# A streaming encoder layer on one core: the norm row stays in PSUM, the first tile's products are reordered, and output weights and gates are staged in other buffers

## The chip, the core and the metric

The kernel runs on 1 NeuronCore of one Trainium2 chip. The engines are TensorE (PE, with its weight loads as PEld), VectorE (DVE), ScalarE (ACT), GpSimd (POOL) and SyncE (SP, which issues all DMAs here). The metric is the device time of one execution in microseconds, as the median of several runs; lower is better.

## The reference

One layer of a hybrid encoder, for 2048 new frames and 64 frames of a running stream with a past of 4096. After a root-mean-square norm one combined projection gives ten column blocks; two branches (differential attention and retention) follow, each gated, projected, weighted by a sigmoid gate and summed; an output projection and the residual close the layer.

```python
h = rmsnorm(x, norm_g) @ w_in                      # 1024 -> 6144 columns
qa, ka, va, za, qb, kb, vb, zb, ga, gb = split(h)  # 512 each, ga and gb 1024
qa, ka = rmsnorm(qa, qn_g), rmsnorm(ka, kn_g)      # per head half of 64
ga, gb = sigmoid(ga + b_gate[0]), sigmoid(gb + b_gate[1])
oa = diff_attention(qa, ka, va)                    # 4 heads, chunk-causal, ALiBi
ob = retention(qb, kb, vb)                         # 4 heads, decay per head
oa = rmsnorm(oa, subln_g) * (1 - lam_init) * silu(za)
ob = rmsnorm(ob) * silu(zb)
m = ga * (oa @ w_o_diff) + gb * (ob @ w_o_ret)
y = x + m @ w_out
```

All inputs and outputs are 32-bit floats. The keys, the values and the retention state are outputs as well.

## The kernel before

**Products in three passes.** Each operand of a large product is split into a high part (fp32r) and the remainder: h is a cast on ScalarE, l = x - h a subtraction on VectorE or GpSimd. A product is then three passes on TensorE: high x high, high x low, low x high. So every weight piece is loaded by SP into a staging buffer, cast on ScalarE, subtracted on VectorE or GpSimd, and its staging buffer is free after that.

**Order of work.** The program is written as generators that a loop in Python runs by priority against estimated engine times (P, A, V, G, ld, and take and give for buffers); this fixes the order of TensorE, ScalarE and VectorE. The order on GpSimd and on SP comes from the framework's scheduler. Each engine then runs its list in order, and a DMA waits on SP for its buffer and also for the DMA eight places earlier.

**Start.** x_prep and x_norm load a tile of x (128 frames x 1024), take the sum of squares on ScalarE (L288), then the inverse root (Ln L291, Exp L292, and small VectorE steps L295 to L300 on one column), and scale x by it and by the norm row gn (L305). gn is norm_g spread over 128 partitions by a product with a matrix of ones (L271) and copied from PSUM into a row buffer (L273). x_tile transposes on TensorE (L319), and casts and subtracts into xh and xl (L326, L327). w_load loads w_in in pieces of 256 KB, w_split casts (L391) and subtracts them (on GpSimd L398, or VectorE L395); natural and mm_group multiply (L427). The first eight pieces have eight staging places (STAGE), of which the first and the last share a pool of three. Twelve small products of ones (L1607) run before x is there.

**Middle.** Projections, attention (z_stream) and retention are interleaved on TensorE until the projections of the second half end with the gate columns gb, which are stored from ev to gbT (L615). z_stream ends some 60 us before the projections; then load_wo loads both 512 x 1024 weights w_o in 32 pieces of 128 x 256 through the nine buffers of oz, and out_prep loads z and o of each branch in groups of 264 frames and forms o * silu(z), split into ogh and ogl (og_fin, L1330 to L1347).

**Output projection.** It starts when the last projection is done, since its buffers (pool p3b: w_out, the gates gt, m, xt, yt) lie where the projection's were. out_stream runs eight groups of 256 prompt frames and 8 sample frames. m_tile makes one of eight blocks of 128 columns for both branches in PSUM (tags mm and s, two buffers each; L1385 to L1387). m_fin multiplies both by their gates on VectorE (L1405), which frees the PSUM, adds them on GpSimd (L1409) and splits the sum (mh L1415, ml L1423). gate_prep loads a pair of gate tiles (ga and gb, 132 KB each) and applies the sigmoid (L1366). load_wout loads w_out in 32 pieces of 128 x 256; these and the gate pairs share the six buffers of gt. y_tile multiplies m by w_out (L1450 to L1452; 8 blocks of m x 2 halves of the columns x 3 passes), and y_fin adds x (L1464) and stores. A last y_tile serves the 64 sample frames.

Of the kernel before, what the change touches and what calls it, by code (L numbers as in the profile page):

```python
# [12 lines left out]
ALU = mybir.AluOpType  # L13
# [22 lines left out]
        "oz": 9, "og": 17, "gt": 6, "m": 18, "xt": 2, "yt": 2}  # L36
# [5 lines left out]
XFLY = 5  # L42
STAGE = ["ws", "ws", "ws", "ath", "ath", "atl", "atl", "ws"]
# [12 lines left out]
class Hybrid:  # L56
# [192 lines left out]
    def x_prep(self, half):  # L249
# [4 lines left out]
        gn = self.row("gn")  # L254
        jk = self.row("xjk")
        tiles = self.xtiles(half)
        left = [len(tiles)]
        for j, (src, r, seg, col) in enumerate(tiles):
            yield lambda: self.xfly < XFLY and (half > 0 or self.wloads >= min(4 * j, 8))
# [5 lines left out]
            if j == 0 and half == 0:  # L265
                tg = self.ld(self.gz[0:1, :], self.i["norm_g"][0:1, :], 4096)
                self.ld(self.ident, self.i["c_ident"], 1 << 16)
                for k in range(2):
                    sl = slice(512 * k, 512 * k + 512)
                    ps = self.psum("s")  # L270
                    nc.tensor.matmul(ps, self.ones, self.gz[:, sl], start=True, stop=True)  # L271
                    t = self.P(2048)
                    nc.vector.tensor_scalar_mul(gn[:, sl], ps, 128.0)  # L273
                    tg = self.V(512, t)
                self.give("row", tg)
# [5 lines left out]
        self.give("row", self.dve + LAT, 2)  # L281

    def x_norm(self, j, xt, jk, gn, t, tg, r, seg, col, left):
# [11 lines left out]
        nc.vector.tensor_scalar(ms, ss, 1.0 / D, EPS, op0=ALU.mult, op1=ALU.add)  # L295
        self.V(1, t)
        yield t2
        nc.vector.scalar_tensor_tensor(out=ms, in0=y, scalar=y, in1=ms, op0=ALU.mult, op1=ALU.mult)
        nc.vector.tensor_scalar(ms, ms, -0.5, 1.5, op0=ALU.mult, op1=ALU.add)
        nc.vector.tensor_mul(y, y, ms)  # L300
# [4 lines left out]
        nc.vector.scalar_tensor_tensor(out=xt, in0=xt, scalar=y, in1=gn[:r], op0=ALU.mult, op1=ALU.mult)  # L305
# [37 lines left out]
    def w_load(self):  # L343
        for half in range(2):
            for c0, wide in self.order[half]:
                for q in range(8 if wide else 4):
                    tag = STAGE[q] if self.wloads < 8 else "ws"
                    yield from self.take(tag)
                    pool = self.wp if tag == "ws" else self.ap
# [31 lines left out]
    def w_split(self):  # L381
        nc = self.nc
        nw = n = 0
        for c0, wide in self.order[0] + self.order[1]:
            for q in range(8 if wide else 4):
# [6 lines left out]
                t = self.A(512, self.pe)  # L392
                if wide and q % 2:
# [7 lines left out]
                if wide:  # L401
                    self.wq.append((h, l, t, tags))
                else:
                    self.wq.append((h[:, 0], l[:, 0], t, ()))
                    self.wq.append((h[:, 1], l[:, 1], t, tags))
# [12 lines left out]
    def mm_group(self, ps, n, us, wsl, x, wfirst, last):  # L418
        nc = self.nc
        seg, xsl = x  # L420
        for c in range(KC):
# [10 lines left out]
            if c % 2 and c < KC - 1:  # L432
                yield self.pe
# [1247 lines left out]
```

## Time and profile before

| what | value |
| --- | --- |
| runs | 2028.14, 2029.12, 2029.59 us; median 2029.12 |
| the profiled execution | 2029.37 us, of which 2027.6 us span |
| TensorE busy | 1991.4 us (98% of the span), 12406 passes |
| VectorE, ScalarE, GpSimd busy | 1003.2, 956.3, 410.5 us |
| DMA | 280.97 MB, mean 139 GB/s |
| mean granted TensorE clock | 0.995 |
| TensorE busy from 0 to 50 us, from 50 to 100 us | 41.81 us (clock 0.90), 48.86 us |
| TensorE busy from 100 to 1600 us | 1493.5 of 1500 us |
| TensorE busy from 1600 to 1650 us, from 1650 to 1700 us | 42.83 us (clock 0.97), 41.77 us (clock 0.93) |
| TensorE busy from 1700 to 2000 us | 49.90 us of each 50 |

How to read it: a line of the timeline gives start and duration in us, the engine, the line of the kernel, the operation, what it writes and from what, and, in brackets, how long the engine had been idle and what ended that. SPq is SP's queue of DMA issues. The span runs from the first to the last instruction; the profiled execution's own time has 1.8 us more.

### The profile page before, as it was taken

How to read it: one execution, taken by the hardware profiler on the slowest of the kernel's cores; microseconds unless marked ns; L12 is line 12 of the kernel's file. 1: busy time of each engine (PE TensorE's matmuls, PEld its weight loads, DVE VectorE, ACT ScalarE, POOL GpSimd, SP SyncE). 2: the span in 40 equal slices, each digit the busy share in tenths (PEclk: the TensorE clock that was granted, in tenths of full speed). 3: DMA queues.
4: the chain of work that ended last, by engine and by line, in shares of the span. 5: the costliest groups of instructions: out<-in, count | busy, mean ns of one | idle time of the engine just before them, and what ended most of it. 6: DMA issues, size and time to landing. Idle time of an engine off the chain costs nothing. (4 is left out here: it accounts for less than half of the span.)

```text
span 2027.6 us, 34426 instructions
## 1 busy us (share of the span) xinstructions
PE 1991.4 (98%) x12406; PEld 1787.8 (88%) x12406; DVE 1003.2 (49%) x2671; ACT 956.3 (47%) x2112; POOL 410.5 (20%) x385
## 2 busy tenths in 40 slices
PE   8999999999999999999999999999999979999999
PEld 6778999989998999999999888888888868888997
DVE  7453566543331421546856555645653455444442
ACT  6332676644332433535666655645653553333321
POOL 2110121121112222221211211122112443222210
PEclk8999999999999999999999999999999989999999
DMA  6646554344565463663352352553234664454531
GB/s 223 200 140 167 149 158 132 106 137 139 152 176 130 135 189 92 180 194 115 115 159 79 96 146 71 148 156 94 68 92 145 187 185 151 142 157 130 149 100 58
DMA packets 332573, 280.97 MB, mean 139 GB/s; under 512 B 64945, under 2 KB 300465, under 8 KB 332402
## 3 DMA queue, kind: packets, MB, share of 16 engines
q1 hardware_dynamic: 332402, 278.77, 46.9%
q8 instruction: 98, 1.61, 0.3%
q14 instruction: 73, 0.60, 0.1%
HBM read 187.19 MB, written 91.49 MB: 137 GB/s over the span
## 5 line engine op out<-in xcount | busy, mean ns | idle before, releaser
L427 PE MATMUL mm<-xh,wh 128*128 128x512 f32 (+2 forms) x1280 | 461.2, 360 | 0.0
L427 PE MATMUL mm<-xh,wl 128*128 128x512 f32 (+2 forms) x1280 | 451.6, 353 | 0.0
L427 PE MATMUL mm<-xl,wh 128*128 128x512 f32 (+2 forms) x1280 | 450.9, 352 | 0.0
L398 POOL TENSOR_TENSOR wl<-ws,wh 128x512 fp32r<-128x512 f32 x180 | 239.3, 1339 | 926.8 <-ACT wh L391 602.5
L427 PE MATMUL mm<-wh,xh 128*128 128x256 f32 (+3 forms) x872 | 276.6, 317 | 0.3 <-DVE tlo L558 0.3
L427 PE MATMUL mm<-wh,xl 128*128 128x256 f32 (+3 forms) x872 | 271.0, 311 | 0.0
L427 PE MATMUL mm<-wl,xh 128*128 128x256 f32 (+3 forms) x872 | 270.8, 311 | 0.0
L427 PEld LDWEIGHTS mm<-xh,wl 128*128 128x128 f32 x1280 | 241.0, 188 | 31.9
L427 PEld LDWEIGHTS mm<-xh,wh 128*128 128x128 f32 x1280 | 241.2, 188 | 29.7 <-issue 0.2
L427 PEld LDWEIGHTS mm<-xl,wh 128*128 128x128 f32 x1280 | 241.5, 189 | 29.0
L615 ACT COPY ev<-mm 128x512 f32<-128x512 f32 x140 | 71.6, 511 | 250.3 <-PE mm L427 232.1
L427 PEld LDWEIGHTS mm<-wh,xh 128*128 128x128 f32 (+1 forms) x872 | 164.6, 189 | 11.7 <-PE s L790 0.4
L427 PEld LDWEIGHTS mm<-wl,xh 128*128 128x128 f32 (+1 forms) x872 | 164.8, 189 | 11.1
L427 PEld LDWEIGHTS mm<-wh,xl 128*128 128x128 f32 (+1 forms) x872 | 164.3, 188 | 10.9 <-DVE xl L327 0.2
L911 DVE TENSOR_TENSOR atl<-at,ath 128x512 fp32r<-128x512 f32 (+1 forms) x144 | 93.6, 660 | 141.3 <-ACT ath L909 141.3
L828 ACT ACTIVATE row<-row,a_mx 128x1024 f32<-128x1024 f32 (+7 forms) x160 | 153.6, 963 | 18.4 <-DVE a_mx L808 18.2
L798 DVE CUSTOM_DVE_ANT_0 row<-s,dfar 128x512 f32<-128x512 f32 (+2 forms) x192 | 117.9, 632 | 74.9 <-PE s L790 73.6
L391 ACT CAST wh<-ws 128x512 fp32r<-128x512 f32 x192 | 116.8, 618 | 45.6 <-PE mm L427 27.5
L909 ACT CAST ath<-at 128x512 fp32r<-128x512 f32 (+1 forms) x144 | 79.5, 563 | 92.5 <-PE at L896 92.1
L789 PE MATMUL s<-K,q 128*128 128x512 f32 (+3 forms) x320 | 120.5, 381 | 2.5 <-DVE a_acc L798 2.5
L790 PE MATMUL s<-K,q 128*128 128x512 f32 (+3 forms) x320 | 115.2, 362 | 0.0
L849 DVE SCALAR_TENSOR_TENSOR row<-row,a_w 128x1024 f32<-128x1024 f32 (+4 forms) x96 | 97.6, 1026 | 28.1 <-ACT row L846 27.9
(201 smaller groups left out, 3946.6 us busy)
## 6 DMA issues: line engine op xcount, KB each, us to landing
ws<-in_w_in_dram SPq DMA_DIRECT2D x192, 256.0 KB, 3.0
q<-qT SPq DMA_DIRECT2D x128, 128.0 KB, 3.0
V<-vN SPq DMA_DIRECT2D x24, 512.0 KB, 5.4
K<-kT SPq DMA_DIRECT2D x48, 256.0 KB, 4.2
gt<-gaT SPq DMA_DIRECT2D x64, 132.0 KB, 2.1
gt<-gbT SPq DMA_DIRECT2D x64, 132.0 KB, 2.1
xt<-in_x_prompt_dram SPq DMA_DIRECT2D x16, 512.0 KB, 6.3
kn<-in_cache_k_T_dram SPq DMA_DIRECT2D x32, 256.0 KB, 3.9
```

The source lines that it names most:

```text
L391: nc.scalar.copy(h, st)
L398: nc.gpsimd.tensor_sub(l, st, h.bitcast(F32))
L427: nc.tensor.matmul(ps, p, q, start=c == 0 and i == 0, stop=c == KC - 1 and i == 2)
L615: nc.scalar.copy(ev, ps)
L789: nc.tensor.matmul(ps, q1s, kk, start=True, stop=False)
L790: nc.tensor.matmul(ps, q2s, kk, start=False, stop=True)
L798: nc.vector.tensor_tensor_reduce(out=units[k0 // 1024][:, k0 % 1024:k0 % 1024 + n], in0=ps, in1=tab, scale=-SLOPES[h], scalar=3.0e38, op0= ...
L828: nc.scalar.activation(u, u, AF.Exp, bias=mx, scale=-1.0, accum_out=lp[:, k:k + 1])
L849: nc.vector.scalar_tensor_tensor(out=u0, in0=u0, scalar=w[:, 0:1], in1=u1, op0=ALU.mult, op1=ALU.add)
L909: nc.scalar.copy(ah[:, :w], at[:, :w])
L911: nc.vector.tensor_sub(al[:, :w], at[:, :w], ah[:, :w].bitcast(F32))
```

## The change

It has four parts.

- **Start.** The spread norm row stays in two PSUM buffers (tag s) and is read there by the scaling of x, in two halves; the product with ones has one row instead of 128, and the factor 128 moves into the inverse root. Ln and Exp are queued directly behind the sum of squares, and the small VectorE steps become operations with scalar operands. Six products of ones run first, and ten single ones behind the spreading. Three tiles of x are in flight instead of five in the first half.
- **First tile.** mm_first runs the two high products (xh and xl by wh) of all eight chunks and then the eight low ones (wl). The eighth piece of the early W is staged in ev. The ninth piece waits until five tiles of x are ready. All pieces of W but two (n = 4 and 6) are subtracted on GpSimd; before, in the three wide chunks every second one was done on VectorE.
- **Output weights.** w_o is loaded by quarters of its columns: the first quarter before the inputs of group 0, the others behind them. w_out is loaded in 16 pieces of 128 x 512, first half first, staged in the four buffers of xt and yt and in four new ones (wst). m_tile and y_tile wait only for the quarter or the half that they read.
- **Gates.** The first three pairs are loaded into buffers of oz and go through the sigmoid before the output projection starts; the others follow through the six buffers of gt, each pair after the one before. og_fin multiplies o by z on GpSimd first, and then by the sigmoid, which is written in place. The sample's y_tile runs all of the first half before the second.

```diff
-        "oz": 9, "og": 17, "gt": 6, "m": 18, "xt": 2, "yt": 2}
+        "oz": 11, "og": 16, "gt": 6, "wst": 4, "m": 18, "xt": 2, "yt": 2}
 LAT = 250.0
...
 QUANT = 6
 
 
-XFLY = 5
-STAGE = ["ws", "ws", "ws", "ath", "ath", "atl", "atl", "ws"]
+XFLY = (3, 5)
+EARLY = 3
+STAGE = ["ws", "ws", "ws", "ath", "ath", "atl", "atl", "ev"]
...
@@ -251,34 +252,53 @@
         self.xq = []
         self.xfly = 0
         yield from self.take("row", 2)
-        gn = self.row("gn")
+        gn = self.row("gn") if half else None
         jk = self.row("xjk")
+        if half == 0:
+            self.give("row", 0.0)
...
-            yield lambda: self.xfly < XFLY and (half > 0 or self.wloads >= min(4 * j, 8))
+            yield lambda: self.xfly < XFLY[half] and (half > 0 or self.wloads >= min(4 * j, 8))
             self.xfly += 1
...
-                tg = self.ld(self.gz[0:1, :], self.i["norm_g"][0:1, :], 4096)
+                yield from self.take("row")
+                gz = self.row("gz")
+                t = self.ld(gz[0:1, :], self.i["norm_g"][0:1, :], 4096)
                 self.ld(self.ident, self.i["c_ident"], 1 << 16)
...
+                gn = [self.psum("s") for _ in range(2)]
+                tg = t + 1200
+                self.spawn(self.spread(gn, gz, t), 10)
             elif j == 0:
                 tg = self.ld(gn, self.i["norm_g"][0].partition_broadcast(128), 1 << 19)
             self.spawn(self.x_norm(j, xt, jk, gn, tx, tg, r, seg, col, left), 1, "w")
             yield self.pe
         yield lambda: left[0] == 0
-        self.give("row", self.dve + LAT, 2)
+        if half == 0:
+            self.give("s", self.dve + LAT, 2)
+        self.give("row", self.dve + LAT, 1 + half)
+
+    def spread(self, gn, gz, t):
+        yield t
+        for k in range(2):
+            yield from self.take("s")
+            self.nc.tensor.matmul(gn[k], self.ones[0:1, :], gz[0:1, 512 * k:512 * k + 512], start=True, stop=True)
+            t = self.P(2048)
+        self.give("row", t)
+        for _ in range(10):
+            yield self.pe
+            self.warm(1)
+
+    def warm(self, n):
+        ps = self.psum("at")
+        for _ in range(n):
+            self.nc.tensor.matmul(ps[:, 0:128], self.ones, self.ones, start=True, stop=True)
+            self.P(512)
 
     def x_norm(self, j, xt, jk, gn, t, tg, r, seg, col, left):
...
@@ -287,22 +307,24 @@
         ss, ms, y = (st[:r, k:k + 1] for k in range(3))
         nc.scalar.activation(jk[:r], xt, AF.Square, accum_out=ss)
         t = self.A(1024, self.pe, 190)
-        yield t
         nc.scalar.activation(y, ss, AF.Ln, scale=1.0 / D, bias=self.epst[:r])
         nc.scalar.activation(y, y, AF.Exp, scale=-0.5)
-        self.A(1, t, 40)
+        self.A(1, 0, 40)
         t2 = self.A(1, 0, 40)
+        yield t
         nc.vector.tensor_scalar(ms, ss, 1.0 / D, EPS, op0=ALU.mult, op1=ALU.add)
         self.V(1, t)
         yield t2
-        nc.vector.scalar_tensor_tensor(out=ms, in0=y, scalar=y, in1=ms, op0=ALU.mult, op1=ALU.mult)
+        nc.vector.tensor_scalar(ms, y, y, ms, op0=ALU.mult, op1=ALU.mult)
         nc.vector.tensor_scalar(ms, ms, -0.5, 1.5, op0=ALU.mult, op1=ALU.add)
-        nc.vector.tensor_mul(y, y, ms)
+        nc.vector.tensor_scalar(y, y, ms, 128.0 if isinstance(gn, list) else 1.0, op0=ALU.mult, op1=ALU.mult)
         for _ in range(3):
             t = self.V(20, t2)
         if tg > self.pe:
             yield tg
-        nc.vector.scalar_tensor_tensor(out=xt, in0=xt, scalar=y, in1=gn[:r], op0=ALU.mult, op1=ALU.mult)
+        for k, g in enumerate(gn if isinstance(gn, list) else [gn]):
+            sl = slice(512 * k, 512 * k + g.shape[1])
+            nc.vector.scalar_tensor_tensor(out=xt[:, sl], in0=xt[:, sl], scalar=y, in1=g[:r], op0=ALU.mult, op1=ALU.mult)
         self.xq[j] = (xt, self.V(1100, t), r, seg, col)
         left[0] -= 1
 
...
@@ -345,8 +367,10 @@
             for c0, wide in self.order[half]:
                 for q in range(8 if wide else 4):
                     tag = STAGE[q] if self.wloads < 8 else "ws"
+                    if self.wloads == 8:
+                        yield lambda: len(self.xt_ready) > 4
                     yield from self.take(tag)
...
@@ -389,8 +413,8 @@
                 if t > self.pe:
                     yield t
                 nc.scalar.copy(h, st)
-                t = self.A(512, self.pe)
-                if wide and q % 2:
+                th = t = self.A(512, self.pe)
+                if n in (4, 6):
                     yield t
                     nc.vector.tensor_sub(l, st, h.bitcast(F32))
                     t = self.V(512, t)
...
@@ -431,6 +455,25 @@
                     self.give(tag, self.pe + LAT)
             if c % 2 and c < KC - 1:
                 yield self.pe
+
+    def mm_first(self, ps, us, r):
+        nc = self.nc
+        xh, xl = self.xh[0], self.xl[0]
+        for c in range(KC):
+            if len(us) <= c:
+                yield lambda: len(self.wq) > 0
+                us.append(self.wq.pop(0))
+            if us[c][4] > self.pe:
+                yield us[c][4]
+            for i, x in enumerate((xh, xl)):
+                nc.tensor.matmul(ps, x[:, c, :r], us[c][0], start=c == 0 and i == 0, stop=False)
+                self.P(512)
+        for c in range(KC):
+            if us[c][2] > self.pe:
+                yield us[c][2]
+            nc.tensor.matmul(ps, xh[:, c, :r], us[c][1], start=False, stop=c == KC - 1)
+            self.P(512)
 
     def natural(self, half, fin, fresh=False, wide=False):
         us = []
@@ -444,8 +487,11 @@
                 if fresh:
                     yield lambda: len(self.xt_ready) > j0 + u
                     yield self.xt_ready[j0 + u]
-                yield from self.mm_group(ps[:r, n * u:n * u + n], n, us, slice(0, n),
-                                         (seg, slice(col, col + r)), False, j0 + u == len(tiles) - 1)
+                if fresh and j0 == 0 and wide:
+                    yield from self.mm_first(ps, us, r)
+                else:
+                    yield from self.mm_group(ps[:r, n * u:n * u + n], n, us, slice(0, n),
+                                             (seg, slice(col, col + r)), False, j0 + u == len(tiles) - 1)
                 if u < len(group) - 1:
                     yield self.pe
             t0 = 1024 * half + 128 * j0 if j0 < 8 else T
...
@@ load_wo, load_wout @@
+
+    def load_wo(self, q):
+        sl = slice(256 * q, 256 * q + 256)
         for br, name in enumerate(("w_o_diff", "w_o_ret")):
             for kt in range(4):
+                h, l, slot = self.wo[br][kt]
+                yield from self.take("oz")
+                s = self.sb(self.z3, [128, GW], "oz", "wst")[:, :256]
+                t = self.ld(s, self.i[name][0, 128 * kt:128 * kt + 128, sl], 1 << 17)
+                self.spawn(self.split_fin("oz", h[:, sl], l[:, sl], s, t, (kt + q) % 3 == 0, slot, q), 2)
+                yield self.pe
 
     def load_wout(self):
         pool = self.z4
         for ct in range(8):
             h = pool.tile([128, 1024], F32R, tag=f"woh{ct}", name=f"woh{ct}")
             l = pool.tile([128, 1024], F32R, tag=f"wol{ct}", name=f"wol{ct}")
+            self.wout.append((h, l, {}))
+        for nh in range(2):
+            sl = slice(512 * nh, 512 * nh + 512)
+            for ct in range(8):
+                h, l, slot = self.wout[ct]
+                k = 8 * nh + ct
+                tag = ("xt", "xt", "yt", "yt")[k] if k < 4 else "wst"
+                yield from self.take(tag)
+                s = self.sb(pool, [128, 512], tag, "wst")
+                t = self.ld(s, self.i["w_out"][0, 128 * ct:128 * ct + 128, sl], 1 << 18)
+                self.spawn(self.split_fin(tag, h[:, sl], l[:, sl], s, t, ct % 4 == 3, slot, nh), 2)
+                if nh == 0:
+                    self.wout_left -= 1
+                yield self.pe
 
     def out_prep(self):
         pa = self.z3
-        yield lambda: len(self.wo[1]) == 4
+        for br, name in enumerate(("w_o_diff", "w_o_ret")):
+            for kt in range(4):
+                h, l = (pa.tile([128, 1024], F32R, tag=f"{name}{n}{kt}", name=f"{name}{n}{kt}") for n in "hl")
+                self.wo[br].append((h, l, {}))
+        yield from self.load_wo(0)
         for g in range(8):
             gsl = slice(GW * g, GW * g + GW)
             for br, (oT, zT) in enumerate(((self.oaT, self.zaT), (self.obT, self.zbT))):
                 for kt in range(4):
-                    yield from self.take("oz", 3)
+                    yield from self.take("oz", 2)
                     on = self.sb(pa, [128, GW], "oz", "on")
                     z = self.sb(pa, [128, GW], "oz", "z")
-                    sg = self.sb(pa, [128, GW], "oz", "sg")
                     self.ld(z, zT[kt][:, gsl], 1 << 17)
                     t = self.ld(on, oT[kt][:, gsl], 1 << 17)
                     og = []
                     self.ogs.append(og)
-                    self.spawn(self.og_fin(on, z, sg, t, og), 1)
+                    self.spawn(self.og_fin(on, z, t, og), 1)
                     yield self.pe
...
+            if g == 0:
+                for ct in range(EARLY):
+                    yield from self.take("oz", 2)
+                    pair = [self.sb(pa, [128, GW], "oz", "gt") for _ in range(2)]
+                    self.spawn(self.gate(0, ct, pair, "oz"), 1)
+                for q in range(1, 4):
+                    yield from self.load_wo(q)
+                yield lambda: self.wout_left == 0
+
+    def og_fin(self, on, z, t, og):
+        nc = self.nc
+        yield t
+        nc.gpsimd.tensor_mul(on, on, z)
+        t = self.G(GW, self.pe)
+        yield t
+        nc.scalar.activation(z, z, AF.Sigmoid)
+        t = self.A(GW, t)
         yield t
         nc.vector.tensor_mul(on, on, z)
         t = self.V(GW, t)
-        self.give("oz", t, 2)
+        self.give("oz", t)
         yield from self.take("og", 2)
...
+    def gate(self, g, ct, pair, tag):
+        for br, gT in enumerate((self.gaT, self.gbT)):
+            t = self.ld(pair[br], gT[ct][:, GW * g:GW * g + GW], 1 << 17)
+        yield t
+        for br in range(2):
+            self.nc.scalar.activation(pair[br], pair[br], AF.Sigmoid, bias=self.bg[:, br, ct:ct + 1])
+            t = self.A(GW, t, 90)
+        self.gts.append((pair, t, tag))
+
     def gate_prep(self):
...
+        yield lambda: len(self.gts) >= EARLY
+        for n in range(EARLY, 64):
+            yield from self.take("gt", 2)
+            pair = [self.sb(self.z4, [128, GW], "gt") for _ in range(2)]
+            yield from self.gate(n // 8, n % 8, pair, "gt")
 
     def m_tile(self, g, ct, og):
...
             for kt in range(4):
                 wh, wl, tw = self.wo[br][kt]
+                yield lambda: ct // 2 in tw
+                ready = tw[ct // 2]
                 if ct == 0:
-                    yield lambda: len(self.ogs) > 8 * g + 4 * br + kt and self.ogs[8 * g + 4 * br + kt] and len(tw) == 4
+                    yield lambda: len(self.ogs) > 8 * g + 4 * br + kt and self.ogs[8 * g + 4 * br + kt]
                     og.append(self.ogs[8 * g + 4 * br + kt][0])
-                    if max(*tw, og[-1][2]) > self.pe:
-                        yield max(*tw, og[-1][2])
+                    ready = max(ready, og[-1][2])
+                if ready > self.pe:
+                    yield ready
                 oh, ol, _ = og[4 * br + kt]
...
-        for ct, nh in [(c, k) for k in range(2) for c in range(7)] + [(7, 0), (7, 1)]:
+        first = 8 if sel is None else 7
+        order = [(c, k) for k in range(2) for c in range(first)] + [(c, k) for c in range(first, 8) for k in range(2)]
+        for ct, nh in order:
             nsl, xt, tx, ps = run[nh]
-            yield lambda: len(self.wout) > ct and len(self.wout[ct][2]) == 4 and len(self.mq[g]) > ct
+            yield lambda: len(self.wout) > ct and nh in self.wout[ct][2] and len(self.mq[g]) > ct
...
                 h, l = sel(h), sel(l)
             wh, wl, tw = self.wout[ct]
-            if max(t, *tw) > self.pe:
-                yield max(t, *tw)
+            if max(t, tw[nh]) > self.pe:
+                yield max(t, tw[nh])
...
+            self.warm(6)
+            self.pe = 0.0
```

More of the change, by code (lines that the diff above doesn't have):

```diff
@@ L421, in mm_group @@
         for c in range(KC):
-            a, b, _, tags = yield from self.w_unit(us, c)
+            a, b, _, tags, _ = yield from self.w_unit(us, c)
             a, b = a[:, wsl], b[:, wsl]
@@ L1593, in run @@
         self.marks = {}
+        self.gts = []
+        self.wout_left = 8
         ET = mybir.EngineType
@@ L1601, in run @@
             nc.vector.memset(self.epst, EPS)
-            self.res["row"].free.pop()
-            self.gz = self.row("gz")
-            nc.gpsimd.memset(self.gz, 0.0)
-            warm = self.psum("at")
-            for _ in range(12):
-                nc.tensor.matmul(warm[:, 0:128], self.ones, self.ones, start=True, stop=True)
-                self.P(512)
+            self.warm(6)
+            self.pe = 0.0
             self.spawn(self.consts(), 0)
```

73 lines of the change are left out of this document (13 added, 60 removed).

## The prediction

> **What bounds it now.** I first read the page: TensorE is busy 98% of the span (1991.4 of 2027.6 us), so little is to be had except where it stands idle or runs at half clock. The table by windows finds those places: the first 60 us, and 1631 to 1674 us, where the output projection begins. The waits view says who is waited for:
>
> ```profile
> PE mm L1385 <- DVE gt L1405: 12.6, 6, 3.9
> PE tp L319 <- DVE xt L305: 5.1, 2, 4.3
> PE at L1450 <- ACT mh L1415: 2.7, 1, 2.7
> ```
>
> Columns: waiter and releaser, us in total, times, longest. Then the second place by windows; the first column after the window is its length, then TensorE's busy time, and the third figure from the right is the granted clock:
>
> ```profile
> 1620.00:1630.00 10.00, 10.00 (x62) 8.99 (x61) 3.49 (x6) 3.19 (x8) 3.69 (x5) 1.00 0.46 139
> 1630.00:1640.00 10.00, 5.96 (x43) 5.54 (x42) 5.72 (x11) 4.99 (x12) 3.25 (x4) 0.95 0.75 224
> 1640.00:1650.00 10.00, 6.87 (x46) 6.44 (x44) 6.17 (x15) 5.46 (x15) 5.86 (x7) 0.88 0.62 181
> 1650.00:1660.00 10.00, 7.43 (x46) 7.22 (x47) 5.55 (x16) 5.28 (x15) 3.35 (x5) 0.83 0.59 179
> 1660.00:1670.00 10.00, 7.16 (x39) 6.53 (x39) 6.86 (x19) 7.31 (x21) 3.14 (x4) 0.83 0.50 152
> 1670.00:1680.00 10.00, 7.29 (x33) 5.62 (x32) 6.28 (x18) 5.27 (x14) 5.41 (x7) 1.00 0.69 203
> ```
>
> In the timeline one turn of this loop reads (start, duration, engine, line):
>
> ```profile
> 1630.68 1.85 SPq L131 DMA_DIRECT2D wst<-in_w_out_dram  x4
> ...
> 1635.48 0.33 SPq L131 DMA_DIRECT2D gt<-gaT  x1
> ...
> 1637.96 0.51 ACT L1366 ACTIVATE gt<-gt,bg 128x264 f32<-128x264 f32 x1
> ...
> 1638.51 0.43 DVE L1405 TENSOR_TENSOR gt<-mm,gt 128x264 f32<-128x264 f32 x1
> ...
> 1639.00 0.59 PE L1385 MATMUL mm<-ogh,w_o_diffh 128*128 128x264 f32 x1 [2.80 <-DVE gt L1405]
> ```
>
> Four pieces of w_out take the buffers that a gate pair needs; the pair is loaded late, its sigmoid and product are late, and TensorE waits for the PSUM that this product empties. Start, the same way:
>
> ```profile
> 7.73 0.14 DVE L295 TENSOR_SCALAR x_st<-x_st 128x1 f32<-128x1 f32 x1
> 8.01 0.53 DVE L298 SCALAR_TENSOR_TENSOR x_st<-x_st 128x1 f32<-128x1 f32 x1
> 8.57 0.15 DVE L299 TENSOR_SCALAR x_st<-x_st 128x1 f32<-128x1 f32 x1
> 8.71 1.26 POOL L398 TENSOR_TENSOR wl<-ws,wh 128x512 fp32r<-128x512 f32 x1 [0.19 <-ACT wh L391]
> 8.76 1.23 DVE L300 TENSOR_TENSOR x_st<-x_st 128x1 f32<-128x1 f32 x1
> 10.03 0.62 ACT L391 CAST wh<-ws 128x512 fp32r<-128x512 f32 x1 [1.39 <-DMA ws<-in_w_in_dram]
> 10.03 1.28 DVE L305 SCALAR_TENSOR_TENSOR xt<-xt,x_st,gn 128x1024 f32<-128x1024 f32 x1
> 11.37 1.12 PE L319 MATMUL tp<-ident,xt 128*128 128x128 f32 x4 [4.28 <-DVE xt L305]
> ```
>
> The sum of squares is there at 5.43 us (Square at 4.28, 1.06, and 0.19 to read it out); the first transposition runs only at 11.37, the first product at 13.16, at half clock (a pass every 0.43 us instead of 0.23).
>
> **Output projection: the loss.** m_tile starts at 1625.78 (call it T0). One m_tile is 24 passes of 0.122 = 2.92 us, eight 23.4. The first y_tile starts at 1667.64, 41.9 after T0: 18.5 lost, which is 12.6 of waits, three half-clock stretches of 3.4 us (half of 10.2 = 5.1), and 0.8 for refilling after waits. In y_tile 2.7 more: 21.2 in all. Later groups repeat every 45.6 us, which is their work, 23.4 + 2 x 48 passes of 0.23.
>
> **Output projection: what stays.** I place the changed kernel's instructions, in the order in which they stand on each engine, with these rows. Pairs 0 to 2 are ready before T0. The last gbT store leaves SP at T0 + 0.8, and pair 3 still waits for it, as the first pair did (issue 1628.85, sigmoid 1632.00, thus T0 + 6.2): done at T0 + 7.1. On ACT, mh of tile 0 stands behind that, and on DVE the second product of tile 1 behind ml of tile 0: T0 + 8.3. Tile 3 needs that PSUM at 8.76 + 1.46 = T0 + 10.2. Next on DVE are three w_out subtractions (0.69 each for this shape at L395), released by casts of pieces issued from T0 + 4.0: ended by T0 + 10.2. Tile 2's product follows at 10.6 to 11.3; tile 4 starts at 11.7. Tile 3's product at 14.0 against 14.6; pair 4 leaves SP behind eight w_out pieces at T0 + 7.6, sigmoid at about 13, needed at 14.6; pair 5's tile must free PSUM by 20.4 and does at about 19. So the eight tiles run through. What is late next is y_tile: on ACT four ogh casts of group 1, which wait for tile 7's end (T0 + 23.4), stand before mh of tile 5, and two sigmoids, three w_out casts and a gate pair before mh of tile 6. It comes at about T0 + 29.5, ml at 30.3, needed at 27.5: 2.9 lost. After a wait of 2.80 the trace has a half-clock stretch (the passes from 1639.00 last 0.42 instead of 0.28 until 1642.2), so 1.7 more; 0.6 for smaller ones. Gain 21.2 - 5.2 = 16. Bounds: 20.5 if y_tile finds all ready; 9 if the w_out pieces land 2 us late and each of tiles 4 to 7 stalls 1.1 (4.4), with one half-clock stretch more (1.7) and 1 on y_tile.
>
> [...]
>
> **Before T0.** W is loaded by quarters, 8 pieces before group 0's inputs and 24 after. Their casts stand between ACT's evacuations of mm, which today keep a beat of 5.44 us (1571.58, 1577.02, 1582.52) with the same casts between. Nothing, then; cost without that cover is rival C.
>
> **Start.** Ln and Exp follow Square: 5.43 + 0.29 + 0.20 = 5.95. Four small DVE operations at about 0.2 end at 6.7; two halves against PSUM at 0.69 (L273 reads this shape from PSUM) end at 8.1 instead of 11.31. On PE stand 6 warm products (12 took 4.32: 2.2), two spreading products (1.88) and 10 warm ones, 3.6 back to back or, as each waits for a forerunner, up to 5.9 at the 0.59 that a first pass after a wait takes: end between 9.0 and 11.3. Transpositions 0.9. The cast of xh also stands behind the fourth weight cast, which ends at 10.65. First product thus at 11.4 to 12.8 (was 13.16). The high products run at full clock, but the order puts tile 1's transpositions before the eighth chunk: Square of tile 1 at 11.8, four casts, halves of xt to 15.7, transpositions to 16.7, low passes to 19.0. Tile 0 ended at 21.27 + 6 x 0.23 = 22.65. Tile 2, which waits for xl, starts at about 30.1 instead of 32.91; after it TensorE is the bound again, so 2.8 would remain, and I take 2.5 for the warm products. Bounds 0 (the ten in the way) and 5 (tile 2's wait of 2.03 and its half-clock stretch gone as well). Ten subtractions go from DVE (0.69) to POOL (1.29): 8 x 1.29 = 10.3 us for a chunk that feeds TensorE for 49 us.
>
> L298 and L300 end when the POOL subtractions beside them do, so the ten moved ones could each hold up a DVE operation by up to 1.29: 13 us at worst, of the 40 in which DVE is idle among the first 100. Hidden, as tiles 0 and 1 meet the same POOL queue as today.
>
> **Tail and middle.** The sample's y_tile runs one half before the other: its last evacuation begins at TensorE's end now as then: 0. In between, the order of interleaved work shifts in places; TensorE idles 6.5 us between 100 and 1600 us, so 0, bounds -2 and +2.
>
> **Sum.** 2029.37 (profiled execution; span 2027.6 and 1.8 around it; 0.25 over the median) - 16 - 2.5 = 2010.9: 2011. Own range: ends -20.5 - 5 and -9 - 0 hardly meet, so 2004 to 2019.
>
> **Rivals.** A measurement of this kernel tells 0.2%, 4.1 us, from no change.
> B, gates still late, 0.14: pairs 3 to 7 go one after another, each behind w_out. If tiles 4 to 7 wait 2.1 each, as the six waits of today do on average, with two half-clock stretches (3.4) and 2.7 on y_tile, 14.5 stay: gain 6.7 + 2.5, 2020. For: gate() loads the next pair only after the last. Against: pairs came every 6.0 us (1635.48 to 1671.55 for six), and at that pace pair 5 is still in time, because three tiles need none.
> C, slower, 0.06: evacuation of mm stuck behind W casts. A store (0.4), four loads (2.0), landing 3.2 (W's median) and four casts (1.2) make 6.8 when strictly in turn, 1.4 over the beat; six beats less one of PSUM buffering is 8.4 - 5.4 = 3.0. It decides from an overrun of 4.0 (24 - 5.4 = 18.6, all of the gain); at 4.5 it gives 2032. Against: the beat holds today.
> D, it does not do what it says, 0.05: the start's gain is eaten by the ten warm products and the projection's by new stalls in the shifted order: 2029.
> Something faster than the range: 0.03.
>
> **Chances.** Forecast 0.72, B 0.14, C 0.06, D 0.05, the rest 0.03. Faster 0.72 + 0.14 + 0.03 = 0.89, lowered to 0.88 for B's far end; same 0.05; slower 0.07. Range 2003 to 2020.
>
> **What would show it.** Right: the wait of mm on gt nearly gone, m_tile's eight in about 24 us, one wait of y_tile on mh of 2 to 3 us; first product before 12.8 at full clock. Wrong: gt still waited for (B), ev late before T0 (C), warm products up to 11 us.

## The result, and the profile after

The changed kernel takes 2018.44 us (median of 6 runs, 2016.98 to 2020.57) against 2029.34 (6 runs of the kernel before, 2027.22 to 2031.80): ratio 0.9947, 95% interval 0.9935 to 0.996. That is 10.9 us faster; 18.4 were forecast. The profiled execution took 2016.98 us, span 2015.2; it is the fastest of the six. The waits view, with the columns of before (waiter and releaser, us in total, times, longest):

```profile
PE at L1516 <- DVE ml L1485: 4.0, 2, 2.1
PE tp L341 <- DVE xl L349: 3.9, 1, 3.9
PE mm L1447 <- DVE gt L1467: 3.7, 3, 1.9
```

The wait of mm on gt fell from 12.6 us to 3.7, the one of the first transposition on xt is gone; y_tile's wait of 2.7 has become 4.0, now for ml on VectorE. The windows of the transition (first figure after the window its length, then busy time of TensorE, weight loads, VectorE, ACT and GpSimd; third figure from the right the granted clock):

```profile
1630.00:1640.00 10.00, 8.06 (x55) 7.85 (x54) 8.25 (x12) 7.32 (x16) 4.99 (x5) 0.85 0.79 262
1640.00:1650.00 10.00, 8.24 (x64) 7.80 (x64) 9.43 (x24) 4.46 (x10) 4.24 (x5) 0.98 0.76 234
1650.00:1660.00 10.00, 7.27 (x40) 5.76 (x39) 8.89 (x17) 7.74 (x20) 5.77 (x7) 1.00 0.88 283
1660.00:1670.00 10.00, 8.67 (x31) 6.80 (x32) 9.68 (x18) 4.74 (x14) 6.80 (x8) 0.83 0.58 177
```

TensorE still stands idle there for 7.8 us, and VectorE is now busy 83 to 97% where it was at 56 to 69%: the work that used to be spread over 48 us has been pressed together. Three marks split the time. T0 is the first m_tile matmul, m the time from there to the first y_tile (23.4 is the work), y from there to group 1's first m_tile (22.1 is the work):

| | T0 | m | y | m + y |
|---|---|---|---|---|
| before | 1625.78 | 41.86 | 25.24 | 67.10 |
| after | 1622.89 | 29.37 | 28.13 | 57.50 |

So 2.9 us came ahead of T0 and 9.6 from the output projection, which still loses 12. The first stall in m_tile, timeline (start, duration, engine, line, what; in brackets the idle time before and its releaser):

```profile
1631.52 1.05 DVE L1323 TENSOR_TENSOR wol<-wst,woh 128x512 fp32r<-128x512 f32 x1 [0.32 <-ACT woh L1316]
...
1632.35 0.62 ACT L1316 CAST woh<-wst 128x512 fp32r<-128x512 f32 x1 [0.86 <-DMA wst<-in_w_out_dram]
...
1634.23 0.69 DVE L1323 TENSOR_TENSOR wol<-wst,woh 128x512 fp32r<-128x512 f32 x1 [0.54 <-ACT woh L1316]
...
1634.97 1.27 POOL L1319 TENSOR_TENSOR wol<-wst,woh 128x512 fp32r<-128x512 f32 x1 [2.95 <-ACT woh L1316]
1635.04 1.23 DVE L1481 TENSOR_TENSOR ms<-gt,ms 128x8 fp32r<-128x8 f32 x1
...
1636.19 0.42 DVE L1467 TENSOR_TENSOR gt<-mm,gt 128x264 f32<-128x264 f32 x1
...
1636.66 0.40 PE L1447 MATMUL mm<-ogh,w_o_diffh 128*128 128x264 f32 x1 [1.94 <-DVE gt L1467]
```

The product that empties PSUM (L1467) stands behind three w_out subtractions, of which each waits for its piece's cast and the cast for its load, and behind an ms of eight columns that takes 1.23 us beside a GpSimd operation and 0.17 without one. TensorE waits 1.94 us and then runs at half clock for 3.4 (the clock of 0.85 from 1630 to 1640). In y_tile, the same view:

```profile
1651.74 1.34 ACT L1405 CAST ogh<-on 128x264 fp32r<-128x264 f32 x4
...
1653.63 0.39 ACT L1477 CAST mh<-gt 128x256 fp32r<-128x256 f32 x1
...
1654.21 2.02 DVE L1408 TENSOR_TENSOR ogl<-on,ogh 128x264 fp32r<-128x264 f32 x4
...
1656.15 1.84 DVE L1397 TENSOR_TENSOR on<-on,z 128x264 f32<-128x264 f32 x2
...
1657.91 0.41 DVE L1485 TENSOR_TENSOR ml<-gt,mh 128x256 fp32r<-128x256 f32 x1
```

mh of tile 5 comes behind group 1's four ogh casts, and its ml behind group 1's ogl and on: 3.9 us between the two. Last the start:

```profile
4.21 3.78 PE L290 MATMUL s<-gz,ones 1*128 1x512 f32 x4 [0.23 <-DMA gz<-in_norm_g_dram]
...
7.92 4.51 PE L300 MATMUL at<-ones 128*128 128x128 f32 x20
8.03 0.75 DVE L327 SCALAR_TENSOR_TENSOR xt<-xt,x_st,s 128x512 f32<-128x512 f32 x1 [0.42 <-PE s L290]
...
12.27 0.60 PE L341 MATMUL tp<-ident,xt 128*128 128x128 f32 x4
...
13.54 0.49 PE L470 MATMUL mm<-wh,xh 128*128 128x512 f32 x1 [0.24 <-ACT xh L348]
```

xt is ready at 8.78, 2.5 us sooner than before, but the transposition stands behind ten warm products (twenty passes) until 12.27, and the first product is at 13.54 (13.16 before).

### The profile page after: what moved, and what is told of

It reads as the page before. It is cut to its first block, busy times and chain, and to the rows that moved or that the text cites. A ratio compares the mean times of both kernels' runs of the same rounds, so it can differ in the third digit from the quotient of the medians.

```text
span 2015.2 us, 34341 instructions
## 1 busy us (share of the span) xinstructions
PE 1991.4 (99%) x12414; PEld 1786.1 (89%) x12414; DVE 992.8 (49%) x2659; ACT 956.9 (47%) x2096; POOL 419.2 (21%) x387
## 3 DMA queue, kind: packets, MB, share of 16 engines
q8 instruction: 98, 1.61, 0.3%
## 5 line engine op out<-in xcount | busy, mean ns | idle before, releaser
L422 POOL TENSOR_TENSOR wl<-ws,wh 128x512 fp32r<-128x512 f32 x190 | 251.9, 1338 | 912.3 <-ACT wh L415 632.2
L451 PE MATMUL mm<-wh,xh 128*128 128x256 f32 (+3 forms) x864 | 272.5, 315 | 0.3 <-DVE tlo L604 0.3
L451 PEld LDWEIGHTS mm<-wl,xh 128*128 128x128 f32 (+1 forms) x864 | 162.7, 188 | 10.6
L451 PEld LDWEIGHTS mm<-wh,xl 128*128 128x128 f32 (+1 forms) x864 | 162.5, 188 | 10.2
```

The costliest lines, as they stand in the source:

```text
L422: nc.gpsimd.tensor_sub(l, st, h.bitcast(F32))
L451: nc.tensor.matmul(ps, p, q, start=c == 0 and i == 0, stop=c == KC - 1 and i == 2)
```

## The experiments

Each kernel is the changed one with the edit shown. Times in us; the ratio is to the kernel before, run on the same chip.

| kernel | median | ratio, 95% interval | T0 | m | y | m + y |
|---|---|---|---|---|---|---|
| output part alone | 2018.98 | 0.9952, 0.9937 to 0.9966 | 1625.10 | 28.89 | 28.81 | 57.7 |
| no ten | 2015.68 | 0.9939, 0.9922 to 0.9955 | 1621.96 | 30.00 | 26.53 | 56.5 |
| no GpSimd | 2018.45 | 0.9953, 0.9938 to 0.9967 | 1622.66 | 26.82 | 32.60 | 59.4 |
| w_out on GpSimd | 2021.73 | 0.9966, 0.9953 to 0.9979 | 1624.15 | 23.64 | 37.40 | 61.0 |
| group 1 late | 2010.44 | 0.9913, 0.9897 to 0.993 | 1622.55 | 28.89 | 22.23 | 51.1 |
| first half on GpSimd | 2020.74 | 0.9969, 0.9956 to 0.9982 | 1622.71 | 23.34 | 36.68 | 60.0 |
| no early pairs | 2022.42 | 0.9973, 0.9963 to 0.9982 | 1624.02 | 37.65 | 24.22 | 61.9 |
| norm late | 2014.09 | 0.993, 0.9915 to 0.9944 | 1620.33 | 30.55 | 26.49 | 57.0 |
| both of the output | 2019.71 | 0.9957, 0.9944 to 0.9971 | 1624.60 | 23.81 | 36.27 | 60.1 |
| all | 2013.97 | 0.993, 0.9917 to 0.9942 | 1618.48 | 23.34 | 36.31 | 59.7 |
| all, twelve warm | 2013.57 | 0.9928, 0.9916 to 0.9941 | 1617.02 | 23.36 | 36.46 | 59.8 |
| gates first | 2019.07 | 0.9957, 0.9943 to 0.9971 | 1621.05 | 25.17 | 36.79 | 62.0 |

**Output part alone.** The start's edits are undone.

```diff
-XFLY = (3, 5)
+XFLY = 5
...
-            self.warm(6)
-            self.pe = 0.0
+            for _ in range(12):
+                nc.tensor.matmul(warm[:, 0:128], self.ones, self.ones, start=True, stop=True)
+                self.P(512)
```

> The output projection as in the changed kernel, the start as before. Theory: the two parts add up. The first m_tile matmul then stands at 1625.8 us again (1622.89 in the changed kernel), the first y_tile 29.4 us after it, and the time is 2018.4 + 2.9 = 2021.3. Rival: the start's 2.9 us are no lasting gain and some other difference ahead of the output projection made them; then the first m_tile matmul stays near 1623 and the time near 2018.4.

T0 is back near the old one and m + y stays at 57.7, so the parts add up in the marks. The median does not show the start's part: 2018.98 is inside the spread of the changed kernel's runs. Seven profiled kernels with the changed start have T0 between 1622.55 and 1624.60, the two with the old one 1625.10 and 1625.78: the start is worth 0.5 to 3.2, by their means 2.1. One profile of each kernel was taken, so a difference in T0 of less than about 2 us between two kernels shows little.

**No ten**, and **norm late** with a second edit:

```diff
-        for _ in range(10):
-            yield self.pe
-            self.warm(1)
...
+        if isinstance(gn, list) and j > 2:
+            yield lambda: len(self.xt_ready) >= j - 1
```

> The changed kernel without the ten warm products behind the spread norm row. Theory S (they stand in the way): xt was ready at 8.78 but the first transposition ran at 12.27; without them it runs at about 9.0, the first product at about 10.6 (behind the fourth weight cast, which ended at 9.95), tile 0 ends some 2 us sooner and the first m_tile matmul comes at about 1621: 2016.5. Rival W (they pay for themselves with the clock): the first product is as early, but its passes last 0.43 us for about 3.4 us more, tile 0 ends where it did, the first m_tile matmul within 0.7 us of 1622.9: 2018 to 2019.

> Without the ten warm products, and with the norm of x tiles 3 to 8 begun only when the tile two before has been transposed, so that on VectorE xl of tile 2 stands ahead of the norm of tile 4 (2.3 us) and not behind it. Theory T (what the earlier first product won was lost again in tile 2's wait for xl: first product 3.6 us sooner, first m_tile matmul only 0.9): that wait falls from 4.67 to about 2.4, the first m_tile matmul comes at 1619 to 1620 (1621.96), 2013.5. Rival U (TensorE waits for the next thing, the norm of tile 4 or a weight chunk): a new wait of 2 us before 60 us, first m_tile matmul at 1622, 2015.7.

Without the ten the first transposition runs at 7.83 and the first product at 9.90, 3.6 us sooner, as S says, though passes take 0.43 us until 12.9, as W says. Of the 3.6, 3.0 are left at tile 2's transposition (23.43 for 26.47), 1.6 at its first product (30.76 for 32.38), and T0 moves by 0.9, nearer to W's 0.7 than to S's 1.9. One wait lies between: tile 3's transposition, placed ahead of tile 2's products, waits 4.67 for xl (3.86 with the ten), because on VectorE xl stands behind the norm of tile 4. With the norm behind it the wait is 1.96 and T0 1620.33: theory T, and rival U's new wait did not come. The two edits took 3.4 us off the time of the changed kernel by the ratios (4.4 by the medians, which are from different chips), and 2.6 off T0: about as much as the start's change had brought.

**No GpSimd** in the first group:

```diff
-                self.spawn(self.split_fin(tag, h[:, sl], l[:, sl], s, t, ct % 4 == 3, slot, nh), 2)
+                self.spawn(self.split_fin(tag, h[:, sl], l[:, sl], s, t, False, slot, nh), 2)
...
+        if g == 0:
+            nc.vector.tensor_add(gs[0], gs[0], gs[1])
+            t = self.V(GW, t)
...
+        if on_dve:
+            nc.vector.tensor_mul(on, on, z)
+            t = self.V(GW, self.pe)
```

> The changed kernel with GpSimd taken out of the first group of the output projection: all sixteen w_out subtractions, the eight sums of gated halves of group 0 and the sixteen products of on and z of groups 1 and 2 run on VectorE. Theory B (VectorE's operations between SBUF tiles wait while a GpSimd operation runs): wol back to 0.69 each, on and ogl to 0.43, ms to 0.17, where they took up to 1.2 beside GpSimd; although 9.6 us of work for group 1 and w_out is added, VectorE is no busier between T0 and T0 + 48, the waits of TensorE there shrink from 7.7 to about 4, 2013 to 2015. Rival L (VectorE has simply too much to do there): its work grows by 9.6 us, the waits grow by at least 4: 2022 or more.

VectorE's groups by form from 1622 to 1682 (name, shape, count, busy us, mean ns, idle before), the changed kernel first, then this one:

```profile
L1397 DVE TENSOR_TENSOR on<-on,z 128x264 f32<-128x264 f32 x17 | 10.7, 645 | 7.5 <-ACT z L1394 7.5
L1323 DVE TENSOR_TENSOR wol<-wst,woh 128x512 fp32r<-128x512 f32 x12 | 10.7, 897 | 2.8 <-ACT woh L1316 2.8
L1467 DVE TENSOR_TENSOR gt<-mm,gt 128x264 f32<-128x264 f32 x8 | 3.4, 424 | 0.0
L1481 DVE TENSOR_TENSOR ms<-gt,ms 128x8 fp32r<-128x8 f32 x8 | 3.4, 420 | 0.3
```

```profile
L1323 DVE TENSOR_TENSOR wol<-wst,woh 128x512 fp32r<-128x512 f32 x16 | 10.9, 689 | 1.2 <-ACT woh L1316 1.1
L1401 DVE TENSOR_TENSOR on<-on,z 128x264 f32<-128x264 f32 x17 | 7.2, 430 | 5.7 <-ACT z L1398 5.7
L1471 DVE TENSOR_TENSOR gt<-mm,gt 128x264 f32<-128x264 f32 x8 | 3.4, 428 | 0.0
L1489 DVE TENSOR_TENSOR ms<-gt,ms 128x8 fp32r<-128x8 f32 x8 | 1.3, 168 | 0.3
```

Sixteen wol cost what twelve did, on is back at 430 ns and ms at 168: VectorE, with 28 operations more on it, is busy 40.4 us of these 60 instead of 42.5. These are the times that B gave to single operations. Its forecast of the kernel's time did not come: m fell to 26.8, but y rose to 32.6, with one wait of 6.05 us for mh of tile 6: its sum, now on VectorE, began at 1657.54, behind w_out subtractions and on products that wait for casts and loads, and its cast came 1.4 us after that sum's end, behind a gate pair on ACT. The speed of VectorE decides only a part.

**W_out on GpSimd**, and **first half on GpSimd**:

```diff
-                self.spawn(self.split_fin(tag, h[:, sl], l[:, sl], s, t, ct % 4 == 3, slot, nh), 2)
+                self.spawn(self.split_fin(tag, h[:, sl], l[:, sl], s, t, True, slot, nh), 2)
```

```diff
-                self.spawn(self.split_fin(tag, h[:, sl], l[:, sl], s, t, ct % 4 == 3, slot, nh), 2)
+                self.spawn(self.split_fin(tag, h[:, sl], l[:, sl], s, t, nh == 0, slot, nh), 2)
```

> The changed kernel with all sixteen w_out subtractions on GpSimd (four now). Theory B (VectorE waits while GpSimd runs): twelve more GpSimd operations of 1.29 us stretch VectorE's remaining ones by as much as the 12 x 0.69 = 8.3 us that it is relieved of; the first y_tile comes no sooner than 29 us after T0, 2018 to 2024. Rival L (VectorE's own load sets the stalls): 8.3 us less on VectorE, the wait of the fifth m_tile (1.94) gone and the eight tiles done within 25 us: 2013 to 2014.

> The changed kernel with the subtractions of w_out's first half on GpSimd and those of the second half on VectorE (a quarter of each on GpSimd now). Theory Q (in m_tile the products that empty PSUM stand behind w_out subtractions on VectorE, whose pieces land late): m_tile's eight in 24 to 25 us, as in the run with all sixteen on GpSimd (23.64), where they took 29.4; the y phase about 28 as in the changed kernel; 2013 to 2014. Rival B (each GpSimd operation stretches VectorE's by as much, so it only moves the loss): y phase 32 to 34, 2018.

Both pairs of theories were half right. With no w_out subtraction of the first half on VectorE the eight m_tiles run through (23.64 and 23.34): those subtractions were the stall in m_tile. But y grows to 37.4 and 36.7, and the sum is worse by 2.5 to 3.5: TensorE reaches y_tile six us sooner and waits there longer. The longest wait of the second kernel is 5.83 us for mh of tile 6, which comes at 1660.69, where the changed kernel has it at 1656.62.

**No early pairs**: EARLY is 0.

> The changed kernel without the three gate pairs that are loaded ahead of the output projection; all pairs then come after the last gbT store through the six gt buffers. Theory E (they carry the first stage): pair 0 is ready 6 to 7 us after T0, the third m_tile waits some 3.5 us and one half-clock stretch follows, m_tile's eight in 33 to 35 us: 2023. Rival F (eight staging buffers for w_out alone, which keep its pieces out of the gt buffers, made the gain): tiles 2 to 7 catch up behind the w_out subtractions that they wait for anyway, 29 to 31 us: 2018 to 2020.

Theory E, with other sizes: the fourth m_tile waits 6.96 us, where 3.5 at the third was expected, and m is 37.65; y is 3.9 shorter than in the changed kernel, so that the time, 2022.42, comes out as expected all the same. The three early pairs are worth 61.9 - 57.5 = 4.4 us of the 9.6; the other 5.2 come with the remaining edits of the output projection, which were not taken apart further.

**Group 1 late**:

```diff
-                yield lambda: self.wout_left == 0
+                yield lambda: self.wout_left == 0 and self.ygo
...
+            self.ygo = True
             for tt in range(2):
```

> The changed kernel with the inputs of group 1 (z, on and their products, sigmoids and splits) held back until the first y_tile begins; in the changed kernel they run from T0 + 5 on. Theory Q (in y_tile mh and ml of tiles 5 and 6 wait behind group 1's ogh casts on ACT and its on and ogl on VectorE, and in m_tile VectorE is slowed by its on): m_tile's eight in 27 to 28 us (29.4), the y phase in 24 (28.1; 22.1 is the work), 2013. Rival R (group 1 is then late itself): a wait of 3 us or more at the first m_tile of group 1, 2017 to 2020.

y is 22.23, the bare work; group 1's first m_tile has no wait. In the waits view of this kernel from 1615 to 1700 only m_tile's is left of the two:

```profile
PE mm L1447 <- DVE gt L1467: 3.5, 2, 2.2
```

m moved by 0.5 only, less than the 1.4 to 2.4 expected. 2010.44 is the best time of the study, 8 us under the changed kernel by the medians and 6.9 by the ratios; m + y is 6.4 shorter. The edit frees ACT, VectorE, GpSimd and SyncE at once (the gate pair of tile 5 leaves SyncE 19.1 us after T0 in the changed kernel, here at 11.1 and 15.9); which of the four counted most is not separated.

**Both of the output, all, all with twelve warm products**: group 1 late and first half on GpSimd; then also the two start edits; then warm(12) for warm(6).

> Both edits of the output projection together: group 1's inputs held back until the first y_tile, and w_out's first half subtracted on GpSimd, its second half on VectorE. Theory Q (two queues, one loss each: w_out subtractions ahead of the PSUM products in m_tile, 5.5 to 6.0 us; group 1 ahead of tiles 5 to 7 in y_tile, 5.7 us): the losses go together, m_tile's eight in 23.4 to 24, the y phase in 22.2 to 23, 2018.4 - 11.5 = 2007, or 2010.4 - 5.5 = 2005 from the run with group 1 held back. Rival B (GpSimd's subtractions are late for y_tile, which started sooner): y phase 26 or more, 2010.

> The former with the start as well: no ten warm products, norm of later x tiles behind the transposition of earlier ones. If the start's gain is kept to the end: the first m_tile matmul at 1620.3 as in that run (1622.89 in the changed kernel), 2.5 us under the kernel with both edits of the output projection, 2002.5 to 2004.5. If the orders it changes on the way cost something: no better than that kernel.

> The former with twelve warm products at the start, as the kernel before has, where there are six. Theory K (six leave TensorE slow: the four products that spread the norm row took 3.77 us, in the kernel before 1.88 behind twelve): the spread takes 1.9 and ends at about 7.2, the first transposition at about 8 at full clock, 0 to 1 us gained at the first m_tile matmul. Rival (the six more products delay the spread by what they save): first transposition at 7.6 to 8.2 as in the run with six, passes of 0.43 us after it, no gain.

Theory Q fell: the two gains do not go together, y is 36 again. SyncE, ACT and TensorE of the first of the three, timeline by engine:

```profile
1641.80 5.13 SPq L132 DMA_DIRECT2D wst<-in_w_out_dram  x4
1647.36 0.33 SPq L132 DMA_DIRECT2D gt<-gaT  x1
...
1655.43 1.32 ACT L1316 CAST woh<-wst 128x512 fp32r<-128x512 f32 x2 [5.43 <-DMA wst<-in_w_out_dram]
1656.66 0.92 ACT L1418 ACTIVATE gt<-gt,bg 128x264 f32<-128x264 f32 x2
...
1659.98 0.80 PE L1514 MATMUL at<-woh,mh 128*128 128x512 f32 x1 [7.26 <-ACT mh L1477]
```

Four w_out pieces hold SyncE for 5.1 us until GpSimd's subtractions free their staging buffers; tile 6's gate pair leaves behind them at 1647.36, and its sigmoid stands on ACT behind two casts that wait 5.4 us for later pieces. Of the 14.2 us that y loses, 9.6 are waits and some 4 are half clock in two stretches after them. Holding a buffer longer on GpSimd (four subtractions in 5.20 us there, 0.69 each on VectorE without GpSimd) cost more than VectorE's time that it saved. The start's edits kept their worth on top: T0 1618.48 for 1624.60, 5.7 us in the median. Twelve warm products spread the norm row in 1.98 us where six took 3.78 (theory K), but the first transposition came no sooner (7.77 for 7.66) and the first products took 0.43 us a pass in both, as the rival says, so nothing is gained that these runs can tell: 2013.57 and 2013.97.

**Gates first**: the last kernel, with pairs 3 to 5 issued together and w_out's second half behind a later pair.

```diff
+            if nh:
+                yield lambda: self.ngate >= 8
...
+            if n < 8:
+                self.spawn(self.gate(0, n, pair, "gt"), 0)
+                yield self.pe
```

> The kernel with both edits of the output projection, the start's two and twelve warm products, and on SyncE gate pairs 3 to 5 issued together ahead of w_out's pieces, and w_out's second half only behind gate pair 6 or 7. Theory G (the y phase of 36 us in the last four kernels with GpSimd subtractions is the gate pair of tile 6, whose load stands on SyncE behind w_out pieces that wait for a free staging buffer: issue at 1654.25, tile 6's matmuls done at about 1645): m_tile's eight in 23.4 to 24.5, the y phase 22.2 to 26, 2013.6 less 10 to 14: 2000 to 2004. Rival P (GpSimd's own queue of subtractions, sums and products sets the pace): the sums of tiles 5 to 7 come late whatever the loads do, y phase 32 or more, 2010 to 2014.

The expectation names 1654.25 as the issue of tile 6's pair; it is that of tile 7's, tile 6's is 1647.36. Theory G fell in its number: mh is no longer waited for, but now woh and wol of w_out's second half are (3.2 and 2.1 us the longest), issued from 1645.99 to 1659.23, as the pair ahead of them waited on SyncE for a buffer behind four GpSimd subtractions (5.17 us in a row). P is right that GpSimd's queue sets the pace, though by what it holds up. The median is 5.5 us above that of the kernel before it, but 4.0 of these stand ahead of T0, which this edit does not touch: with the same start, tile 3's transposition waits 3.22 us for xl where it waited 1.61, and a half-clock stretch follows (a pass every 0.43 us from 30.11 to 33.53, every 0.23 there in the other). That is how far two profiles of one start can differ. Group 1 late with the two start edits, without GpSimd's half, was not tried.

## Why the prediction was right, and where it was not

The direction was right, the size too large: in the profiled pair 12.4 us were gained instead of 18.4, by the medians 10.9. The time lies in the stated range, near its slow end, and that owes something to the width of the range: of the signs named for being right only the full clock at the first product (granted clock 1.00 from 12.2 to 20 us) came whole. The wait on gt kept 3.7 us, the eight m_tiles took 29.4 and not 24, y_tile had two waits for ml instead of one for mh, and the first product came at 13.54, not before 12.8.

**What bounds it, before T0, tail.** Right. ACT's evacuations keep their beat of 5.44 us up to T0 (1617.70, 1623.14), so rival C fell. From group 1's first m_tile to the end both kernels take 334.7 to 334.8 us, so nothing is left for the tail; the marks give 2.9 + 9.6 = 12.5 of the 12.4. The middle, put at 0, gave 1.1: TensorE idles 5.4 us between 100 and 1600 where it idled 6.5 (4.7 to 6.1 in the seven kernels with this start, 6.3 and 6.5 in the two with the old one).

**Output projection, m_tile: the step that was mis-sized.** "So the eight tiles run through" took 18.5 us of loss to nothing; 6.0 stayed: waits 3.7, half of one half-clock stretch 1.7, refilling 0.6. It rests on "three w_out subtractions ... ended by T0 + 10.2". They ended at T0 + 12.0, since their pieces came 1.2 to 1.5 us apart (casts at 1630.87, 1632.35, 1633.58) and not at the 0.5 of their issue; then the ms of 1.23 us, and the product of tile 2 stood at T0 + 13.3, forecast at 10.6 to 11.3. Three more subtractions followed, two of them 2.93 us beside GpSimd. The prediction had seen L298 and L300 end with the GpSimd subtractions beside them (0.53 and 1.23 us, without one 0.21 to 0.22 and 0.16), and priced it for the start alone. Both GpSimd runs show the cause: without those subtractions on VectorE m is 23.3 to 23.6. GpSimd has a part in it: with all subtractions on VectorE and GpSimd almost idle m is 26.8, so 2.6 of the 6.0 go with GpSimd.

**Output projection, y_tile.** 5.2 was forecast, 28.13 - 22.1 = 6.0 measured. One wait of 2.9 us for tile 6 was forecast; two came, 2.08 for ml of tile 5 and 1.87 for ml of tile 6, and the half-clock stretch with them. That stretch was less certain than the step made it: in the same trace of before, the wait of 2.71 us in y_tile has none behind it. The ogh casts ahead of mh of tile 5 were there as described; the larger part is the ogl and on between mh and ml on VectorE, which the step left out. Group 1 late shows that holding group 1 back ends the whole of it, y 22.23, though not through which queue.

**Start.** 2.5 forecast, 2.9 in this pair: a good sum from wrong parts, and so luck. The sum of squares and the halves came as worked out, to 0.7 us (8.78 for 8.1); the second half waited for the spread. The ten warm products ended at 12.4, outside the 9.0 to 11.3: the six took 2.93 and not 2.2, since half the time of twelve is not that of the first six (of the twelve in the kernel before a pass takes 0.21 us until 3.78 and 0.11 from 3.98 on), and the spread took 3.78 and not 1.88. Tile 2 started at 32.38, not at 30.1, 0.5 sooner than before. The other 2.4 us came later, from what the sum had not priced: two waits for xl after 50 us (0.66 and 0.34 before, gone now) and the 1.1 us of the middle.

**Rivals.** B was closer than its 0.14 said: 2020 against 2018.4. Its waits of tiles 4 to 7 are three of 0.6 to 1.9 us, for products that stand behind w_out on VectorE more than for gates; the gates become the limit as soon as m_tile runs through. D fell.

## What to carry to other kernels

When a wait is removed, place the whole of the work that follows on every in-order queue, with landing times of the loads and not their issue times; a loss of 12 us that four queues share moves on when one of them is relieved. Holding back the next stage's inputs, which costs three short lines, won more here than any finer division of the work on the output projection. An earlier first instruction is worth what the next wait leaves of it: 3.6 us at the first product were 0.9 at T0 until tile 2's wait was cut.

## What the runs showed of the hardware

**VectorE beside GpSimd.** Some operations whose inputs are all in SBUF took longer beside a GpSimd operation. In the changed kernel ms (L1481) took 0.17 us in the 57 that overlapped none and up to 1.23 in the seven that overlapped one by over 0.1 us; on (L1397) 0.42 to 0.44 in 41 and up to 1.52 in 21; the cast ms (L1480, one input) 0.16 to 0.17 in 57 and up to 0.72 in six. The products gt (L1467), which read PSUM, took 0.42 to 0.43 in the 17 that overlapped one by over 0.1 us. Nor was the scaling of xt in the second half (L327, 128x1024, inputs in SBUF) longer: 1.28 to 1.29 in six without and two beside one.

**The clock at the start.** With six warm products (2.93 us) the spread took 3.77 to 3.78 us in nine kernels, but 2.07 in "first half on GpSimd", whose start is that of six of them; there the first product came at 11.26, and T0 was 1622.71 all the same. Behind twelve, which took 4.83 us in "all, twelve warm" and 5.49 in "gates first", it took 1.98. Why one start had two outcomes the runs do not show.

**Half clock after short waits.** In m_tile a single wait of 1.94 us was followed by a stretch of 3.4 us at half clock (passes of 0.22 us, 0.12 elsewhere), as were those of 2.12 (no ten), 2.19 (group 1 late) and 2.80 (before), while waits of 1.28 (group 1 late) and 1.62 (no early pairs) were not. The length of a wait does not decide alone: the 2.71 us in y_tile of the kernel before had no stretch behind it, and a wait of 2.03 us near 31 us had one in the kernel before and none in "output part alone".
